# Attention operands without the norm row, head 1 in block form, two weight chunks split by an adding transfer

## The chip, the cores and the metric

One core of a Trainium2 chip. The metric is the device time of one execution in microseconds (us), median over runs. In the rows PE is TensorE (PEld its weight loads), DVE VectorE, ACT ScalarE, POOL GpSimd, SP SyncE; SPq, ACTq and POOLq are the DMA queues that SP, ACT and POOL issue to. L12 is line 12 of the kernel; one line's number differs a little between the kernel before and the changed one.

## The reference, cut to what matters

512 tokens of 1024 features, float32, two layers: dilated attention and a SwiGLU FFN, then a pooling mixer and a SwiGLU FFN, a root-mean-square norm ahead of each. The change touches the attention only:

```python
def rmsnorm(x, g):
    y = x * lax.rsqrt(jnp.mean(x * x, axis=-1, keepdims=True) + RMS_EPS)
    return y * g

# mixer A, h = rmsnorm(x, g): 8 heads of 128, three groups with (window, dilation)
#   (128, 1), (512, 4), (2048, 16); each group has its own q, k, v
qkv = (h @ w_qkv).reshape(B, S, 3, 3, 8, 128)
for g in range(3):
    o[g], lse[g] = dilated_window_attention(q[g], k[g], v[g], window, dil, slopes[g])
    # s = q k^T / sqrt(128) - slope * distance, masked; p = softmax(s); o = p v
wts = softmax(lse over the three groups)
out = sum(wts * o) @ w_out ; x = x + out
```

The norm's factor per token, 1 / sqrt(mean(x^2) + eps), is called the row here. q, k and v are linear in h, so it may be applied to x ahead of the product or to the result behind it.

## The kernel before

x stands transposed: eight tiles `X[c]` of 128 features by 512 tokens. A float32 product is made of two float32r parts of each factor, high and low (`split`: high part by ScalarE at L92, low part by VectorE as the difference at L93), and three matmuls: high by high, high by low, low by high.

**Plain products** (`Product`, matmuls at L329, L330, L332): one output chunk of 128 x 512 takes 8 feature chunks by three matmuls of 128x512. L332 is the one that reads the weights' low part. **Block form** (`seven`, matmuls in `mult` at L461 to L463): two output chunks at once from seven products of half-size blocks, 7 x 4 x 3 = 84 matmuls of 128x256, whose results VectorE adds together at L502 to L516. Its operands are sums of blocks of h, kept in `T` and made by `normed` and `prepare`. The weights of a block-form pair (`Pair`) come in two whole raw tiles and a half, one of which gets the fourth corner added by a transfer from GpSimd's queue (L173); sums of blocks are made by VectorE (L189, L190). A plain chunk with `lean` (used later in the kernel, L146 to L149) has its low part made otherwise: ScalarE writes the high part, then minus the high part, and a transfer on GpSimd's queue adds the weight from memory to that.

**The start.** x and the first weights (`w_first`) arrive chunk by chunk; the four lead products (L933, 96 matmuls) follow them on operands `U` without the row (x times the gain `nrm`). Squares of x are summed by TensorE (L411), VectorE forms `var` (L414), GpSimd takes the power (L417, `rcol`, per-token scalars on partitions), and `spread` (TensorE, L424) with an ACT copy (L942) makes `rows["row"]`, the row on all partitions. Meanwhile two further plain chunks of head 0 (`begin`) run. `prepare(k)` makes the block-form operands from x times gain times row, after the row is there. Of 24 qkv pairs most are in block form; head 0 is plain (6 q/k chunks, 2 v chunks), and so are head 1's first two groups (`NSOLO`).

**A head.** For each group g `seven` makes q and k; steps of earlier heads run between its products (`between`): `scores0` (group 0, L719), `scores12` (groups 1 and 2, L736, L740, L743), `scatter`, `merge` (weights `co` of the three groups; s0 scaled by DVE at L783, s12 by ACT at L786), `turn0` and `turn12` (transposes), `output` (L841, 30 small matmuls per head). v of two heads comes at once: group 0 in even heads (turned by `turn_values`), groups 1 and 2 in odd heads (`values12`). After head 7 the plain and block-form products with `w_out` follow, with `output` of heads 6 and 7 among them.

Loads are issued on SP's queue in the order of use, from rings of tiles (`raw` 4, `w` 5, `half` and `rawhalf` 2); `pump` splits the next weights. A scheduler orders each engine's instructions; on each engine they run in that order.

Of the kernel before, what the change touches and what calls it, by code (L numbers as in the profile page):

```python
# [8 lines left out]
F32 = mybir.dt.float32  # L9
# [6 lines left out]
P = 128  # L16
S = 512
# [25 lines left out]
NSOLO = 2  # L43
# [22 lines left out]
def trunk(ctx: ExitStack, tc: tile.TileContext, xT, xN, norms, w_first, w_qk, w_qkp, w_v0, w_v0p, w_v12, w_out, w_outp, w_pair, w_down, w_dblock, w_pin, w_pgrp,  # L66
# [173 lines left out]
    for h in range(HEADS):  # L240
        if h == 0:
            plain(*[w_qk[u] for u in range(len(QK) - NF)])
        for g in range(3):
            if h == 1 and g < NSOLO:
                plain(*[w_qk[len(QK) - NF + 2 * g + c] for c in range(2)])
            elif h:
                pairs(w_qkp[3 * h - 3 - NSOLO + g])
        if h == 0:
            plain(w_v0[0], w_v0[1])
        elif h % 2 == 0:  # L250
            pairs(w_v0p[h // 2 - 1])
        else:
            pairs(w_v12[h // 2, 0], w_v12[h // 2, 1], shift=APART)
# [216 lines left out]
    def seven(T, one, two, scratch, after={}, blocks=False):  # L470
# [44 lines left out]
        nc.vector.tensor_sub(into(two), p45, again(sums[:, :H2]))  # L515
        nc.vector.tensor_sub(into(one, right), sums[:, H2:], p45[:, H2:])  # L516
        behind(6)
# [56 lines left out]
    def normed(layer, k, row, h, t, chained=False):  # L574

        for i in range(2):
            c = k + i * K2
            nc.vector.scalar_tensor_tensor(h.t[:, i * S:(i + 1) * S], X[c], nrm[:, layer, c:c + 1], row,
                                           op0=OP.mult, op1=OP.mult)
# [20 lines left out]
    with tc.tile_pool(name="opool", bufs=1) as opool:  # L600
        early = [opool.tile([P, 2, S], F32R, tag=f"o{k}", name="early") for k in range(K2)]
        with tc.tile_pool(name="apool", bufs=1) as apool:
# [6 lines left out]
            def scaled_by(t, p, blocks):  # L609
                nc.vector.tensor_mul(by_block(t) if blocks else t, p, rows["row"])  # L610

            def evac(h, u, p):
                g, c = QK[u]
                t = apool.tile([P, S], F32, name=f"qk{g}{c}")
                scaled_by(t, p, g == 0)
                QKV[h, g, c] = t

            def values12(after={}):
# [59 lines left out]
                behind(6)  # L678
                return t
# [3 lines left out]
            def turn_values(h):  # L683

                t = apool.tile([P, NT, 2 * P], F32, name="v0")
                for c in range(2):
                    p = ps()
                    for b in range(NT):
                        nc.tensor.transpose(blk(p, b), blk(VT[c], b), ident)
                    nc.scalar.copy(t[:, :, c * P:(c + 1) * P], p.rearrange("p (b d) -> p b d", b=NT))  # L690
# [5 lines left out]
            def scores0(h):  # L696
# [12 lines left out]
                for blocks, bias in (((1, 2, 3), b0[:, :G]), ((0,), b0[:, G:])):  # L709
                    p = ps()  # L710
                    for i, b in enumerate(blocks):
# [6 lines left out]
                    n = len(blocks)  # L718
                    nc.vector.scalar_tensor_tensor(  # L719
                        s0[:, blocks[0]:blocks[0] + n], p[:, :n * G].rearrange("p (a k) -> p a k", a=n), SCALE,  # L720
                        bias[:, None].to_broadcast([P, n, G]), op0=OP.mult, op1=OP.add)
# [7 lines left out]
            def scores12(h):  # L729
# [4 lines left out]
                p, n = ps(), ps()  # L734
                for r in range(NT):
                    nc.tensor.matmul(blk(p, r), blk(QKV[h, 1, 0], r), blk(QKV[h, 1, 1], r), start=True, stop=True)  # L736
                for r in range(NT):
                    for j in range(NT):
                        c = slice(j * NI, (j + 1) * NI)
                        nc.tensor.matmul(n[c, r * NI:(r + 1) * NI], blk(QKV[h, 2, 0], r)[:, c], blk(QKV[h, 2, 1], r)[:, c],  # L740
                                         start=True, stop=True)
                for b, p, k in ((b12[:, :P], p, slice(0, P)), (b12[:, P:], n[:, :P], slice(P, G))):
                    nc.vector.scalar_tensor_tensor(  # L743
                        s12[:, :, k], p.rearrange("p (r k) -> p r k", r=NT), SCALE,
                        b[:, None, :].to_broadcast([P, NT, b.shape[1]]), op0=OP.mult, op1=OP.add)
# [15 lines left out]
            def merge(h):  # L761
# [20 lines left out]
                for b in (1, 2, 3, 0):  # L782
                    nc.vector.tensor_scalar(s0[:, b], s0[:, b], co[:, 0, b:b + 1], None, op0=OP.mult)  # L783
# [47 lines left out]
            def output(h):  # L831
# [21 lines left out]
                for r in range(NT):  # L853
# [4 lines left out]
            late = [apool.tile([P, S], F32R, tag=tag, name="early") for tag in ("t0", "o0")]  # L858
            late12 = apool.tile([P, 2, S], F32R, tag="t12", name="early")
            latev = apool.tile([P, 4, S], F32R, tag="v12", name="early")  # L860
            U = ([(early[k][:, 0], early[k][:, 1]) for k in range(K2)]
                 + [(latev[:, 2 * k], latev[:, 2 * k + 1]) for k in range(2)]
                 + [(late12[:, 0], late12[:, 1]), tuple(late)])
            H, T, o = {}, {}, []
# [667 lines left out]
```

## Time and profile before

| | |
|---|---|
| median of 3 runs | 1185.67 us (1185.33 to 1185.95) |
| the profiled execution | 1186.22 us, span 1184.4 us, clock 0.999 |
| busy: PE, DVE, ACT, POOL | 1175.3, 984.0, 721.8, 171.0 us |
| attention | to about 430 us; the rest is output projection, FFNs and the pooling mixer |
| DMA | 207.57 MB, mean 175 GB/s |

The page's group rows read: line, engine, operation, output from input, count, then busy time, the mean of one in ns, and the idle time before it with what ended it. A timeline row reads: start, duration, engine, line, operation, and in brackets how long the engine had been idle and what released it. A row with "from to" windows gives the length, and for each engine its busy time and instruction count, then the granted clock, the DMA share and GB/s.

### The profile page before, as it was taken

What the parts mean: (1) busy time and instruction counts of PE and PEld (TensorE: products, weight loads), DVE (VectorE), ACT (ScalarE), POOL (GpSimd) and SP (SyncE); (2) the same over time, 40 slices, a digit from 0 to 9 for tenths busy, and PEclk for the clock granted to TensorE, in tenths of its full rate; (3) what the DMA queues carried; (4) which work ended last, traced back from release to release, by engine and by line L of the source; (5) the groups of instructions that cost most, each with busy time, mean ns of one, the idle gap of its engine ahead of it and who ended that gap; (6) DMA issues with size and microseconds to landing.
All of it is one profiled execution on the core that took longest, in us unless ns stands there. A gap on an engine that the chain in (4) does not pass through costs nothing.

```text
span 1184.4 us, 25169 instructions
## 1 busy us (share of the span) xinstructions
PE 1175.3 (99%) x10042; PEld 1120.1 (95%) x10042; DVE 984.0 (83%) x1725; ACT 721.8 (61%) x1262; POOL 171.0 (14%) x165
## 2 busy tenths in 40 slices
PE   9999999999999999999999999999999999999997
PEld 7889999999999989889999999988889999999997
DVE  7997898879789878699988988656789998898875
ACT  6554554546455557747756775775575776676553
POOL 1101111111111002311111111122130111111100
PEclk9999999999999999999999999999999999999999
DMA  8537667665766557957777777798595777777732
GB/s 299 133 96 186 147 154 166 168 160 149 194 145 163 146 156 198 252 104 202 189 190 193 195 197 199 195 266 207 121 203 111 189 193 202 194 192 192 198 91 72
DMA packets 83766, 207.57 MB, mean 175 GB/s; under 512 B 7856, under 2 KB 13120, under 8 KB 83648
## 3 DMA queue, kind: packets, MB, share of 16 engines
q1 hardware_dynamic: 52672, 144.84, 36.4%
q0 software_dynamic: 30688, 60.83, 31.6%
q8 instruction: 78, 1.28, 0.4%
q14 instruction: 40, 0.33, 0.1%
q10 hardware_dynamic: 288, 0.29, 0.1%
HBM read 203.84 MB, written 2.10 MB: 174 GB/s over the span
## 4 chain that ended last, share of the span: by engine, by line
PE 96%; DMA 2%; issue 1%; DVE 1%; ACT 0%; POOL 0%; POOLq 0%; DVEq 0%; ACTq 0%
PE ps L461 21%; PE ps L463 20%; PE ps L462 20%; PE ps L329 7%; PE ps L330 7%; PE ps L332 7%; PE ps L841 2%; PE ps L933 2%; PE ps L632 2%; PE ps L634 2%; PE ps L633 2%; DMA raw<-w_outp 1%; PE ps L716 1%; PE ps L736 1%; PE ps L424 0%
## 5 line engine op out<-in xcount | busy, mean ns | idle before, releaser
L92 ACT ACTIVATE w<-raw 128x1024 fp32r<-128x1024 f32 x268 | 283.6, 1063 | 172.7 <-PE ps L463 67.5
L93 DVE TENSOR_TENSOR w<-raw,w 128x1024 fp32r<-128x1024 f32 x268 | 326.4, 1222 | 55.3 <-ACT w L92 51.2
L461 PE MATMUL ps<-far,w 128*128 128x256 f32 x896 | 246.5, 275 | 0.0
L462 PE MATMUL ps<-far,w 128*128 128x256 f32 x896 | 246.5, 275 | 0.0
L463 PE MATMUL ps<-far,w 128*128 128x256 f32 x896 | 246.4, 275 | 0.0
L461 PE MATMUL ps<-near,w 128*128 128x256 f32 x676 | 190.5, 282 | 0.0
L462 PE MATMUL ps<-near,w 128*128 128x256 f32 x676 | 186.9, 277 | 0.0
L463 PE MATMUL ps<-near,w 128*128 128x256 f32 x676 | 186.9, 276 | 0.0
L462 PEld LDWEIGHTS ps<-far,w 128*128 128x128 f32 x896 | 168.2, 188 | 0.1
L461 PEld LDWEIGHTS ps<-far,w 128*128 128x128 f32 x896 | 168.2, 188 | 0.1
L463 PEld LDWEIGHTS ps<-far,w 128*128 128x128 f32 x896 | 168.2, 188 | 0.0
L461 PEld LDWEIGHTS ps<-near,w 128*128 128x128 f32 x676 | 127.1, 188 | 0.5
L462 PEld LDWEIGHTS ps<-near,w 128*128 128x128 f32 x676 | 127.1, 188 | 0.0
L463 PEld LDWEIGHTS ps<-near,w 128*128 128x128 f32 x676 | 127.0, 188 | 0.0
L329 PE MATMUL ps<-near,w 128*128 128x512 f32 (+1 forms) x316 | 119.4, 379 | 0.0
L332 PE MATMUL ps<-near,w 128*128 128x512 f32 (+1 forms) x316 | 118.7, 376 | 0.0
L330 PE MATMUL ps<-near,w 128*128 128x512 f32 (+1 forms) x316 | 118.7, 376 | 0.0
L173 POOL DMA_DIRECT2D raw<-w_pair x36 | 43.6, 1210 | 296.5 <-DMA raw<-w_pair 131.8
L329 PEld LDWEIGHTS ps<-near,w 128*128 128x128 f32 x316 | 59.3, 188 | 10.9 <-ACT near L92 0.4
L332 PEld LDWEIGHTS ps<-near,w 128*128 128x128 f32 x316 | 59.3, 188 | 10.9
L330 PEld LDWEIGHTS ps<-near,w 128*128 128x128 f32 x316 | 59.5, 188 | 10.7 <-DVE near L93 0.2
L92 ACT ACTIVATE half<-rawhalf 128x512 fp32r<-128x512 f32 x84 | 52.8, 630 | 14.0 <-PE ps L463 11.8
(328 smaller groups left out, 2784.8 us busy)
## 6 DMA issues: line engine op xcount, KB each, us to landing
raw<-w_pair SPq DMA_DIRECT2D x80, 512.0 KB, 5.0
raw<-w_qkp SPq DMA_DIRECT2D x38, 512.0 KB, 4.6
raw<-w_pair POOLq DMA_DIRECT2D x36, 512.0 KB, 7.6
raw<-w_dblock SPq DMA_DIRECT2D x32, 512.0 KB, 4.5
raw<-w_qkp POOLq DMA_DIRECT2D x19, 512.0 KB, 7.6
raw<-w_v SPq DMA_DIRECT2D x18, 512.0 KB, 4.5
rawhalf<-w_pair SPq DMA_DIRECT2D x36, 256.0 KB, 5.2
raw<-w_dblock POOLq DMA_DIRECT2D x16, 512.0 KB, 7.4
```

Of the source, the lines that this page charges most:

```text
L92: nc.scalar.activation(hi, v, AF.Copy)
L93: nc.vector.tensor_tensor(lo, v, hi.bitcast(F32), op=OP.subtract)
L173: nc.gpsimd.dma_start(self.b.rearrange("p (a c) -> p a c", a=2), self.src[:, None, 3 * n:].to_broadcast([P, 2, n]), accum_op=OP.add)
L329: nc.tensor.matmul(self.p[:, cols], w[0][:, s], mh[:, cols], start=self.done == 0, stop=False)
L330: nc.tensor.matmul(self.p[:, cols], w[0][:, s], ml[:, cols], start=False, stop=False)
L332: nc.tensor.matmul(self.p[:, cols], w[1][:, s], mh[:, cols], start=False, stop=self.done == self.n)
L461: nc.tensor.matmul(dst, w.t[0][:, c], th, start=k == 0 and not on, stop=False, skip_group_check=on)
L462: nc.tensor.matmul(dst, w.t[0][:, c], tl, start=False, stop=False, skip_group_check=on)
L463: nc.tensor.matmul(dst, w.t[1][:, c], th, start=False, stop=k == n - 1, skip_group_check=on)
L632: nc.tensor.matmul(o, mh, wh, start=k == 0, stop=False)
L633: nc.tensor.matmul(o, mh, wl, start=False, stop=False)
L634: nc.tensor.matmul(o, ml, wh, start=False, stop=k == K2 - 1)
```

## The change

- Operands without the row. `U` (the leads' operands, high and low of x times gain) serve as the block-form operands for T11, T21 and T22; `prepare` no longer splits h (two chunks of it a call, four calls), and scales x on ScalarE (L576) with no wait for the row. `prepare(0)` moves ahead of `rstd`.
- The row is multiplied in behind the products. The second output of `seven` (k, or the second v chunk) by VectorE (L513, new, with the subtraction at L511 now in place); the first (q) not at all: its factor goes into the scale of the scores, per-token scalars `rk`, so that the scores' scale and bias takes four VectorE operations of 128x160 each instead of one or two larger ones (L721, L746). v of group 0 is scaled in `turn_values`' copies, v of groups 1 and 2 by four ScalarE operations of 128x512 in place (L680).
- `rk` is made from `rcol` by eight tiny ScalarE copies (L948) and, in the other order of tokens, by four one-column matmuls (L944) from `line`, a ScalarE copy of one partition of the row (L942).
- Head 1's groups 0 and 1 and the v pair of heads 0 and 1 go to block form; the plain weights `w_v0` and two plain pairs of `w_qk` are gone.
- The two plain q/k chunks of head 0 are `lean`: low part by ScalarE and an adding transfer.
- The scaling of s0 in `merge` goes from VectorE to ScalarE (L785).

```diff
-            plain(*[w_qk[u] for u in range(len(QK) - NF)])
+            plain(*[w_qk[u] for u in range(len(QK) - NF)], lean=True)
 ...
-        nc.vector.tensor_sub(into(two), p45, again(sums[:, :H2]))
         nc.vector.tensor_sub(into(one, right), sums[:, H2:], p45[:, H2:])
+        nc.vector.tensor_sub(p45 if row is not None else into(two), p45, again(sums[:, :H2]))
+        if row is not None:
+            nc.vector.tensor_mul(into(two), p45, row)
 ...
+            if row is None:
+                nc.scalar.activation(h.t[:, i * S:(i + 1) * S], X[c], AF.Copy, scale=nrm[:, layer, c:c + 1])
 ...
             def evac(h, u, p):
-                nc.vector.tensor_mul(by_block(t) if blocks else t, p, rows["row"])
+                if c:
+                    nc.vector.tensor_mul(v, p, rows["row"])
+                else:
+                    nc.scalar.copy(v, p if g else p.rearrange("p (y x z) -> p y x z", y=Y16, z=2))
 ...
             def values12(after={}):
+                for r in range(NT):
+                    nc.scalar.activation(t[:, r], t[:, r], AF.Copy, scale=rk[:, 1, r:r + 1])
 ...
             def scores0(h, ...):
-                    nc.vector.scalar_tensor_tensor(
-                        s0[:, blocks[0]:blocks[0] + n], ..., SCALE, ...)
+                    for i, b in enumerate(blocks):
+                        nc.vector.scalar_tensor_tensor(s0[:, b], p[:, i * G:(i + 1) * G], rk[:, 2, b:b + 1], bias,
+                                                       op0=OP.mult, op1=OP.add)
 ...
             def merge(h):
                 for b in (1, 2, 3, 0):
-                    nc.vector.tensor_scalar(s0[:, b], s0[:, b], co[:, 0, b:b + 1], None, op0=OP.mult)
+                    nc.scalar.activation(s0[:, b], s0[:, b], AF.Copy, scale=co[:, 0, b:b + 1])
 ...
             def prepare(k):
-                h, t = normed(0, k, rows["row"], Room(), Temp())
-                for i in range(2):
-                    held["h", k + i * K2], b = slot("h")
-                    H[k + i * K2] = b[:, 0], b[:, 1]
-                    split(*H[k + i * K2], h.t[:, i * S:(i + 1) * S])
-                T["11", k] = halves_of(*H[k])[0]
-                T["21", k], T["22", k] = halves_of(*H[k + K2])
+                h, t = normed(0, k, None, Room(), Temp())
+                T["11", k] = halves_of(*U[k])[0]
+                T["21", k], T["22", k] = halves_of(*U[k + K2])
 ...
+            lead += begin(1, 0, range(2))
+            prepare(0)
             rcol = rstd([acc[0]])
-            lead += begin(1, 0, range(3))
+            lead[-1].add(range(2, 5))
             nc.scalar.activation(rows["row"], spread(rcol), AF.Copy)
-            lead[-1].add(range(3, KC))
+            lead[-1].add(range(5, KC))
+            p, line = ps(), scratch("line")
+            nc.scalar.copy(line[:1].rearrange("p (x y z) -> p x y z", y=Y16, z=2), in_a_row(rows["row"][:1]))
+            for b in range(NT):
+                nc.tensor.matmul(p[:, b:b + 1], blk(line, b)[:1], ones[:1], start=True, stop=True)
+            for i, scale in ((0, 1.0), (2, SCALE)):
+                nc.scalar.activation(rk[:, i], p[:, :NT], AF.Copy, scale=scale)
+                for t, c in enumerate(rcol):
+                    nc.scalar.activation(rk[:, i + 1, t:t + 1], c, AF.Copy, scale=scale)
 ...
-            for h in range(1, HEADS):
-                for g in range(3):
+            for h in range(HEADS):
+                for g in range(3 if h else 0):
 ...
-                        seven(T, QKV[h, g, 0], QKV[h, g, 1], scratch, between(h, g), g == 0)
+                    seven(T, QKV[h, g, 0], QKV[h, g, 1], scratch, between(h, g), g == 0, rows["row"])
```

How the order of the instructions changes, at the places that the prediction speaks of. First GpSimd's queue at the start, before (`b` tiles are the scores' bias, `var` the mean square, `rcol` its power):

```order
L702 TENSOR_SCALAR b_492<-const 128x320
L705 TENSOR_SCALAR b_494<-const 128x128
L705 TENSOR_SCALAR b_494<-const 128x32
L417 TENSOR_TENSOR rcol<-var,nhalf 128x2 x2
L173 DMA raw<-w_qkp 128x2x512
L173 DMA raw<-w_v 128x2x512
```

The same queue in the changed kernel:

```order
L705 TENSOR_SCALAR b_518<-const 128x320
L708 TENSOR_SCALAR b_520<-const 128x128
L708 TENSOR_SCALAR b_520<-const 128x32
L148 DMA w<-w_qk 128x1024
L172 DMA raw<-w_v0p 128x2x512
L148 DMA w<-w_qk 128x1024
L172 DMA raw<-w_qkp 128x2x512
L412 TENSOR_TENSOR rcol<-var,nhalf 128x2 x2
```

Four transfers stand ahead of the power that gives the row, where none did.

VectorE around `var` at the start, before (`sq` sums of squares, `w` low parts of plain chunks):

```order
L384 TENSOR_TENSOR sq<-sq 128x512 x2
L93 TENSOR_TENSOR w<-raw,w 128x1024 x4
L414 TENSOR_SCALAR var<-ps 128x4
L93 TENSOR_TENSOR w<-raw,w 128x1024
L578 SCALAR_TENSOR_TENSOR room<-x,nrm,row 128x512 x2
```

And in the changed kernel (`temp`, `near` block sums of the operands; `raw<-raw` differences of the v0 pair's weights):

```order
L92 TENSOR_TENSOR near<-temp,near 128x512 x2
L92 TENSOR_TENSOR w<-raw,w 128x1024
L92 TENSOR_TENSOR half<-rawhalf,half 128x512
L188 TENSOR_TENSOR raw<-raw 128x512
L582 TENSOR_TENSOR temp<-room 128x2x256
L92 TENSOR_TENSOR w<-raw,w 128x1024
L409 TENSOR_SCALAR var<-ps 128x4
L189 TENSOR_TENSOR raw<-raw 128x512
```

`var` now stands behind a subtraction (L188) that reads the tile to which GpSimd's second transfer adds.

ScalarE in the attention's tail, before (`ex` the merge's exponentials, `s` scores, `oh`, `near`, `half` operands and weights of the output projection):

```order
L777 ACTIVATE ex<-ex 128x16
L92 ACTIVATE w<-raw 128x1024 x2
L92 ACTIVATE oh<-room 128x512
L786 ACTIVATE s_5242<-s_5242,co 128x160 x4
L92 ACTIVATE half<-rawhalf 128x512 x2
L92 ACTIVATE near<-room 128x512
L855 COPY o<-ps 128x512
```

And in the changed kernel:

```order
L779 ACTIVATE ex<-ex 128x16
L91 ACTIVATE w<-raw 128x1024 x2
L785 ACTIVATE s_5244<-s_5244,co 128x160 x4
L788 ACTIVATE s_5473<-s_5473,co 128x160 x4
L680 ACTIVATE v_5445<-v_5445,rk 128x512 x4
L91 ACTIVATE oh<-room 128x512
L91 ACTIVATE half<-rawhalf 128x512 x2
L91 ACTIVATE near<-room 128x512
L857 COPY o<-ps 128x512
```

Eight more operations stand between the second weight chunk and `oh`, among them the scaling of the values that `output` reads.

More of the change, by code (lines that the diff above doesn't have):

```diff
@@ L241, in trunk @@
         if h == 0:
-            plain(*[w_qk[u] for u in range(len(QK) - NF)])
+            plain(*[w_qk[u] for u in range(len(QK) - NF)], lean=True)
         for g in range(3):
[L244 to L251, printed above, removed]
+            if h:
+                pairs(w_qkp[3 * h - 3 + g])
+        if h % 2 == 0:
+            pairs(w_v0p[h // 2])
         else:
@@ L468, in part, with seven @@
         return unit.w[name]
-    def seven(T, one, two, scratch, after={}, blocks=False):
+    def seven(T, one, two, scratch, after={}, blocks=False, row=None):
         (unit,), = units.popleft()
@@ L600, in trunk @@
     with tc.tile_pool(name="opool", bufs=1) as opool:
-        early = [opool.tile([P, 2, S], F32R, tag=f"o{k}", name="early") for k in range(K2)]
         with tc.tile_pool(name="apool", bufs=1) as apool:
@@ L855, in output @@
                 nc.scalar.copy(o[h], po)
[L858 to L864, printed above, removed]
+            U, T, o = {}, {}, []
             class Room:
```

96 lines of the change are left out of this document (39 added, 57 removed).

## The prediction

> **What bounds the kernel now.** I read the page first, then the waits of TensorE's queue, then one stretch of two attention heads.
>
> ```profile
> span 1184.4 us, 25169 instructions
> PE 1175.3 (99%) x10042; PEld 1120.1 (95%) x10042; DVE 984.0 (83%) x1725; ACT 721.8 (61%) x1262; POOL 171.0 (14%) x165
> PE 96%; DMA 2%; issue 1%; DVE 1%; ACT 0%; POOL 0%; POOLq 0%; DVEq 0%; ACTq 0%
> PE ps L841 <- ACT t L808: 1.4, 1, 1.4
> PE ps L913 <- DVE idle L910: 1.2, 1, 1.2
> 131.60:233.80 102.20, 102.20 (x1115) 101.54 (x1105) 84.70 (x151) 53.81 (x106) 16.32 (x16) 1.00 0.67 163
> ```
>
> PE (TensorE) is 99% busy, the chain that ended last is 96% PE, and PE has two waits worth naming, both small. Two heads (131.6 to 233.8) take 102.2 us, all of it PE, with VectorE at 84.7, ScalarE at 53.8, and a granted clock of 1.00. So a matmul less is time less, and every new wait of PE is time more: nothing after it makes up for it.
>
> **The change: matmuls.** Three pairs of output chunks (head 1's first two groups, the v0 chunks of heads 0 and 1) go from plain (48 matmuls of 128x512) to block form (84 of 128x256).
>
> ```profile
> 416.15 0.39 PE L329 MATMUL ps<-oh,w 128*128 128x512 f32 x1
> 420.03 0.39 PE L332 MATMUL ps<-near,w 128*128 128x512 f32 x1
> 180.29 0.28 PE L461 MATMUL ps<-near,half 128*128 128x256 f32 x1
> 190.83 0.28 PE L632 MATMUL ps<-w,near 128*128 128x256 f32 x1
> ```
>
> The first two are the ends of a run of 18 plain matmuls: 3.88 us over 17 steps, 0.228 each. The other two stand 93 steps apart: 10.54 us, 0.1133 each. A pair falls from 48 x 0.228 = 10.95 to 84 x 0.1133 = 9.52 us; three pairs give 4.3 us. This is certain as long as PE is fed. Nine transposes or score matmuls more or less don't show; the four small matmuls that make `rk` (L944, one row by 128 columns) have no row in before: nearest is 32 of the sum's 128x1 in 0.43 us (next fence), so 0.05 to 0.5; I take 0.25, since they come in a switch of operands.
>
> **The front.** These are the rows around the first products.
>
> ```profile
> 5.43 22.08 PE L933 MATMUL ps<-early,w 128*128 128x512 f32 x96
> 18.16 0.64 ACT L382 ACTIVATE sq<-x 128x512 f32<-128x512 f32 x1
> 18.70 1.99 ACT L92 ACTIVATE w<-raw 128x1024 fp32r<-128x1024 f32 x2
> 27.44 0.43 PE L411 MATMUL ps<-ones,sq 128*32 128x1 f32 x32
> 27.95 0.16 DVE L414 TENSOR_SCALAR var<-ps 128x4 f32<-128x4 f32 x1 [2.00 <-PE ps L411]
> 28.20 2.23 POOL L417 TENSOR_TENSOR rcol<-var,nhalf 128x2 f32<-128x2 f32 x2 [7.76 <-DVE var L414]
> 28.37 0.39 PE L332 MATMUL ps<-early,w 128*128 128x512 f32 x1
> 29.98 1.21 PE L424 MATMUL ps<-ident,rcol 128*128 128x128 f32 x8
> 30.94 0.48 PE L329 MATMUL ps<-early,w 128*128 128x512 f32 x1
> 31.22 0.60 ACT L942 ACTIVATE row<-ps 128x512 f32<-128x512 f32 x1 [2.62 <-PE ps L424]
> L147 ACT ACTIVATE w<-w 128x1024 fp32r<-128x1024 f32 x32 | 33.6, 1055 | 0.6
> DMA to landing us min/median/max: 5.8/8.2/13.7
> raw<-w_v POOLq DMA_DIRECT2D x1, 512.0 KB, 7.1
> 24.72 1.22 DVE L93 TENSOR_TENSOR w<-raw,w 128x1024 fp32r<-128x1024 f32 x1 [0.23 <-ACT w L92]
> ```
>
> The first leads run until 27.5 and PE goes straight on. The fifth product's weights are split at 18.70 by ScalarE, and their low part by VectorE (1.22 a chunk), long before. Now that low part is made by ScalarE writing minus the high part (1.06, the L147 row, where the kernel does so already) and a transfer issued on GpSimd's queue that adds the weight (L148). ScalarE starts it later too, behind a new scaled room and a zeroed tile (128x512 each, 0.54 to 0.64 by the rows at 18.16 and 18.70): 18.70 + 1.15 = 19.85, high and low part done at 21.9, transfer issued then. Landing of such adding transfers (call it L): the line with the minimum, of the L149 transfers later in the kernel, says 5.8 to 13.7, median 8.2; the one of a v chunk in the first 60 us took 7.1. I take L = 7.6, between the two.
>
> 1. The third matmul of the fifth product (L327) needs it, two matmuls after the leads' end, at 27.9, and all later matmuls stand behind it: a wait of 21.9 + L - 27.9 = 1.6.
> 2. GpSimd issues behind it (23.0) the adding transfer of the v0 pair, which also lands after L. VectorE subtracts from what it brings (L188) ahead of `var` (L409): about half of 1.22 each for that and the temp, 1.22 for a chunk's low part, so `var` starts at 23.0 + L + 2.5 instead of 27.95. From `var` to the end of the spread matmuls was 2.97 (27.95 to 30.94, all in the rows). PE has 1.36 us more work before the spread than it had (six more plain matmuls): it would have been through at 32.3. Now 25.5 + L + 3.0 = 36.1, so 3.8 later in all, wait 1 included.
> 3. The `rk` matmuls wait for `line`, a copy of the row's first partition. On ScalarE, between `rcol` and `line`: eight tiny `rk`, a chunk's high part (1.06), two 128x512 splits, the row (0.60), a room (0.6), the copy (at most 0.6), some 4.7 us; PE has the spread and nine matmuls ahead of it, 2.5 us. A further wait of 2.0, between 1.2 (were the small ones free) and 2.8.
>
> Front: 3.8 + 2.0 + 0.25 = 6.05, or L - 1.55. While PE stands there, VectorE and ScalarE gain slack, but PE cannot make it up. What the operands save elsewhere (the row's split of eight h tiles, 0.6 to 0.7 each on both engines) lies beside PE work.
>
> GpSimd's queue order is the heart of this. The Trainium skill, "DMA: Bandwidth & Descriptors", section "Anatomy of one DMA — SWDGE (gpsimd) path", fits such a transfer as 2.0 us plus bytes over 436e3, 3.2 us for 512 KB (my estimate from it). By that, wait 1 would be nil and wait 2 too; the rows (5.8 at the least, 7.1 here) disagree with it by a factor of two.
>
> **Through the heads.** The place to watch is an odd head's scores of groups 1 and 2, where PE reads the second output of a pair soon after it is made; the rows are of such a place.
>
> ```profile
> 191.97 0.68 DVE L515 TENSOR_TENSOR qk<-ps,sums 128x512 f32<-128x512 f32 x1
> 192.57 0.41 DVE L516 TENSOR_TENSOR qk<-sums,ps 128x256 f32<-128x256 f32 x1
> 193.60 1.05 PE L736 MATMUL ps<-qk,qk 128*128 128x128 f32 x8
> 194.58 0.46 PE L740 MATMUL ps<-qk,qk 128*32 128x32 f32 x32
> ```
>
> Per pair of heads VectorE gets six row multiplications (0.68 as in the first row) and some 1.2 of smaller splits of its score operations, less eight scalings of 0.23 to 0.3 that ScalarE takes (L783 in the next fence): about +3 on 84.7. ScalarE gets those eight, four 128x512 scalings for an odd head's values and twice four smaller ones: about +6 on 53.8. Of 102.2, both stay beside PE. The second output was ready at 192.6. After the change the order is 0.34, 0.6, 0.69: ready at 193.6 to 194.2, with the group-2 matmuls at 194.6. I price it at nothing; were the cover gone, it is up to 0.6 for each of four odd heads.
>
> **The tail of the attention (head 7).** Here the last two output steps stand before plain products.
>
> ```profile
> 408.84 11.57 DMA raw<-w_outp
> 415.45 0.93 DVE L783 TENSOR_SCALAR s<-s,co 128x160 f32<-128x160 f32 x4
> 418.03 0.69 DVE L677 TENSOR_TENSOR v<-ps,sums 128x512 f32<-128x512 f32 x1
> 420.26 3.51 PE L841 MATMUL ps<-t,v 128*128 128x128 f32 x30
> 420.48 1.06 ACT L92 ACTIVATE w<-raw 128x1024 fp32r<-128x1024 f32 x1 [6.46 <-DMA raw<-w_outp]
> 421.44 0.61 ACT L92 ACTIVATE oh<-room 128x512 fp32r<-128x512 f32 x1
> 421.96 1.37 ACT L786 ACTIVATE s<-s,co 128x160 f32<-128x160 f32 x4
> 423.24 1.14 ACT L92 ACTIVATE half<-rawhalf 128x512 fp32r<-128x512 f32 x2
> 422.71 0.69 DVE L93 TENSOR_TENSOR oh<-room,oh 128x512 fp32r<-128x512 f32 x1
> 426.40 0.43 DVE L1034 TENSOR_TENSOR room<-room,o 128x256 f32<-128x256 f32 x1
> 430.19 3.67 PE ps L841 x30
> ```
>
> ScalarE sits 6.46 us on a chunk whose adding transfer takes 11.57 us to land. In the changed order that chunk stands ahead of four scalings of s0 (L785, VectorE's L783 before), four of s12 (L788) and four of the values (L680, new). From 420.48: chunk to 421.44, two stretches of 1.28 to 424.0, four 128x512 at 0.52 to 426.1 (425.1 if the scalings run closer). Output 6 needs the values after 14 of its 30 matmuls, at 421.8, so PE stands there. `oh`, behind them on ScalarE, goes from 421.44 to 426.1; VectorE's chain after it (oh, a half, a sum, four transposes, L1023, which was L1034) starts at 426.75 instead of 422.71 and reaches L1023 at 429.8 instead of 426.40, and output 7 (L841, at 430.19) hangs on that by the same steps as before. Later by 2.4 to 3.4; I take 2.9. If the transfer lands as in the L149 row (8.2), ScalarE is through before and it costs 0.3.
>
> **The sum.** -4.3 + 6.05 + 2.9 = +4.65, on the profiled execution's 1186.22 us, which is 0.55 above the median: 1190.9 there, 1190.3 as a median.
>
> **Rivals.** (a) The short landing, on the faster side: the adding transfers land in under 3.8 us, and waits 1 and 2 are nil. Front 2.25, tail 0.3: -1.75; with the wait for `line` also covered (its low end 1.2 and the tiny operations hidden), -3.7. So 1182 to 1184, taken as 1182.6. For it speaks only that page's fit; against it that no row goes below 5.8. It decides where L is under 3.8 and the `line` wait under 1.6. (b) Half covered: L at its least, 5.8, and the tail's transfer ahead of need: -4.3 + 4.25 + 0.3 = +0.25, 1185.9. For it: the front's queue holds only two adding transfers by then, and the 11.57 at the tail was with eight loads of x beside it. (c) VectorE decides in the heads: the second outputs come late for the scores, 4 x 0.6 = 2.4 more, 1192.7. For it, 87.6 of 102.2 and a margin of nearly nothing; against it, VectorE waits for ScalarE in between. (d) The block form gives nothing because its weights come late (PE would show waits on L456 to L458 in head 1): +4.3, 1194.6. Against it: 102.2 of 102.2 busy in the same form.
>
> **Chances.** Within 0.2% (2.4 us) is what a measurement here cannot tell from no change. Forecast 0.56, (a) 0.07, (b) 0.24, (c) 0.10, (d) 0.03. Faster 0.07 is (a); same 0.25 is (b) with a little of the forecast's lower end; slower 0.68. The forecast's own range is L from 7.1 to 8.2 and the tail from 0.3 to 3.4: 1187.2 to 1191.4. The 80% range goes from the middle of (a)'s upper edge, 1184, to between (c) and (d), 1194.
>
> **What the changed profile shows.** Waits of PE: a row of L327 on the transfer of w_qk near 1.6; one of the spread (L419) near 2.2; one of L944 on ScalarE's `line` near 2; L843 at the tail on ScalarE's L680 some 3. If L944's and L419's rows are missing, step 2 or 3 is wrong; if PE's windows of two heads grow past 102.2 by over 0.5, (c) is at work. The prediction goes wrong above all if the landing is not near 7.6, on which it hangs one for one.

## The result, and the profile after

The changed kernel takes 1200.26 us (median of 4, 1199.55 to 1201.55), the kernel before 1185.81 in the same runs: ratio 1.0124, 95% interval 1.0106 to 1.0141. It is 14.5 us slower; 4.6 were forecast. The page of the changed kernel, against the rows shown of before:

```profile
span 1199.8 us, 25528 instructions
PE 1180.0 (98%) x10158; PEld 1125.4 (94%) x10158; DVE 993.6 (83%) x1745; ACT 753.5 (63%) x1343; POOL 174.4 (15%) x170
PE 83%; DVE 7%; DMA 6%; issue 2%; ACT 1%; POOL 1%; DVEq 0%; SPq 0%; POOLq 0%; ACTq 0%
```

The chain that ended last, 96% PE before, now runs through VectorE and transfers for 13% of the span. What PE waits for (the waits of its queue: in total, times, longest):

```profile
PE ps L327 <- DMA w<-w_qk: 5.3, 1, 5.3
PE ps L743 <- DVE qk L513: 1.6, 2, 0.9
PE ps L944 <- ACT line L942: 1.5, 1, 1.5
PE ps L843 <- ACT v L680: 1.3, 1, 1.3
PE ps L905 <- DVE idle L902: 1.2, 1, 1.2
PE ps L843 <- ACT t L810: 1.0, 1, 1.0
PE ps L419 <- POOL rcol L412: 0.8, 2, 0.7
```

All the places of the prediction are there, the first three times its size. Two windows, the wait of L327 and what follows it (busy time of PE, PEld, DVE, ACT, POOL, then granted clock, DMA share, GB/s):

```profile
27.50:33.40 5.90, 0.60 (x4) 0.18 (x2) 0.69 (x1) 1.81 (x3) 1.21 (x1) 0.90 1.09 254
33.40:38.90 5.50, 5.50 (x43) 4.09 (x44) 2.31 (x3) 2.31 (x4) 0.00 (x0) 0.50 1.10 229
```

PE is busy all of the second window, but at a granted clock of 0.50. Start by start, 128x512 matmuls there stand 0.427 us apart instead of 0.228. The DMA engines are full (share over 1) while they move 229 to 254 GB/s; before, with loads alone, the same stretch moved 347 to 400 (26.9 to 29.4 us, share 1.02). The rows on GpSimd's queue, VectorE and PE there:

```profile
22.22 1.07 POOL L148 DMA_DIRECT2D w<-w_qk  x1 [1.60 <-ACT w L146]
22.98 1.59 POOL L172 DMA_DIRECT2D raw<-w_v0p  x1
33.40 0.80 PE L327 MATMUL ps<-near,w 128*128 128x512 f32 x1 [5.30 <-DMA w<-w_qk]
36.59 0.69 DVE L188 TENSOR_TENSOR raw<-raw 128x512 f32<-128x512 f32 x1 [7.78 <-DMA raw<-w_v0p]
38.94 0.15 DVE L409 TENSOR_SCALAR var<-ps 128x4 f32<-128x4 f32 x1
45.57 1.05 PE L944 MATMUL ps<-ones,line 1*128 1x1 f32 x8 [1.53 <-ACT line L942]
46.55 0.50 PE L324 MATMUL ps<-near,w 128*128 128x512 f32 x1
```

The first adding transfer, issued at 22.22, releases PE 11.1 us later; the second, issued at 22.98, releases VectorE at 36.5, after 13.5.

**Where the 15.4 us of span went.** Output 0 starts 9.6 us later than before, output 6 13.85, output 7 15.5, and from there to the end the distance stays at 15.4. So the loss lies wholly in the attention. The 48th plain matmul behind the leads starts at 51.90 instead of 39.66, so 12.2 us are lost in the front. From there to output 0, where the three pairs stand, only 2.6 of the 4.3 saved come back, so heads 0 and 1 lose 1.7 if the 4.3 is right. Heads 2 to 7 lose 4.2 and the tail 1.7.

### The profile page after: what moved, and what is told of

It reads as the page before. It is cut to its first block, busy times and chain, and to the rows that moved or that the text cites. A ratio compares the mean times of both kernels' runs of the same rounds, so it can differ in the third digit from the quotient of the medians.

```text
span 1199.8 us, 25528 instructions
## 1 busy us (share of the span) xinstructions
PE 1180.0 (98%) x10158; PEld 1125.4 (94%) x10158; DVE 993.6 (83%) x1745; ACT 753.5 (63%) x1343; POOL 174.4 (15%) x170
## 4 chain that ended last, share of the span: by engine, by line
PE 83%; DVE 7%; DMA 6%; issue 2%; ACT 1%; POOL 1%; DVEq 0%; SPq 0%; POOLq 0%; ACTq 0%
PE ps L456 19%; PE ps L458 18%; PE ps L457 18%; PE ps L324 6%; PE ps L327 6%; PE ps L325 6%; DMA raw<-w_v 2%; PE ps L843 2%; DVE w L92 2%; PE ps L632 2%; PE ps L634 2%; PE ps L633 2%; DMA raw<-w_v0p 1%; DMA raw<-w_outp 1%; DVE half L92 1%
## 5 line engine op out<-in xcount | busy, mean ns | idle before, releaser
L92 DVE TENSOR_TENSOR w<-raw,w 128x1024 fp32r<-128x1024 f32 x269 | 328.5, 1223 | 55.2 <-ACT w L91 50.9
L456 PE MATMUL ps<-far,w 128*128 128x256 f32 x896 | 246.5, 275 | 0.0
L458 PE MATMUL ps<-far,w 128*128 128x256 f32 x896 | 246.4, 275 | 0.0
L456 PE MATMUL ps<-near,w 128*128 128x256 f32 x749 | 210.9, 282 | 0.0
L458 PE MATMUL ps<-near,w 128*128 128x256 f32 x749 | 207.0, 276 | 0.0
L457 PE MATMUL ps<-near,w 128*128 128x256 f32 x749 | 206.9, 276 | 0.0
L456 PEld LDWEIGHTS ps<-far,w 128*128 128x128 f32 x896 | 168.2, 188 | 0.1
L458 PEld LDWEIGHTS ps<-far,w 128*128 128x128 f32 x896 | 168.2, 188 | 0.0
L456 PEld LDWEIGHTS ps<-near,w 128*128 128x128 f32 x749 | 140.7, 188 | 0.5
L457 PEld LDWEIGHTS ps<-near,w 128*128 128x128 f32 x749 | 140.8, 188 | 0.0
L458 PEld LDWEIGHTS ps<-near,w 128*128 128x128 f32 x749 | 140.8, 188 | 0.0
L327 PE MATMUL ps<-near,w 128*128 128x512 f32 (+1 forms) x332 | 126.1, 380 | 5.3 <-DMA w<-w_qk 5.3
L324 PE MATMUL ps<-near,w 128*128 128x512 f32 (+1 forms) x332 | 127.0, 383 | 0.0
L325 PE MATMUL ps<-near,w 128*128 128x512 f32 (+1 forms) x332 | 125.7, 378 | 0.0
L327 PEld LDWEIGHTS ps<-near,w 128*128 128x128 f32 x332 | 62.8, 189 | 17.4 <-DMA w<-w_qk 5.7
L325 PEld LDWEIGHTS ps<-near,w 128*128 128x128 f32 x332 | 63.0, 190 | 11.5 <-DVE near L92 0.2
L324 PEld LDWEIGHTS ps<-near,w 128*128 128x128 f32 x332 | 62.8, 189 | 11.6 <-ACT near L91 0.4
L188 DVE TENSOR_TENSOR raw<-raw 128x512 f32<-128x512 f32 x87 | 59.5, 684 | 10.7 <-DMA raw<-w_v0p 7.8
```

Of the source, the lines that this page charges most:

```text
L92: nc.vector.tensor_tensor(lo, v, hi.bitcast(F32), op=OP.subtract)
L188: nc.vector.tensor_add(a[:, :n], a[:, :n], b[:, :n])
L324: nc.tensor.matmul(self.p[:, cols], w[0][:, s], mh[:, cols], start=self.done == 0, stop=False)
L325: nc.tensor.matmul(self.p[:, cols], w[0][:, s], ml[:, cols], start=False, stop=False)
L327: nc.tensor.matmul(self.p[:, cols], w[1][:, s], mh[:, cols], start=False, stop=self.done == self.n)
L456: nc.tensor.matmul(dst, w.t[0][:, c], th, start=k == 0 and not on, stop=False, skip_group_check=on)
```

## The experiments

Times are medians; the control is the changed kernel, run once more with the second group.

**1. No adding transfers for the two plain chunks.**

```diff
-            plain(*[w_qk[u] for u in range(len(QK) - NF)], lean=True)
+            plain(*[w_qk[u] for u in range(len(QK) - NF)])
```

> Changed kernel, but the two plain chunks of head 0 have their low part made by VectorE as before (no adding transfers for them). Theory A (the late adding transfers at the front and the half clock behind the wait are most of the loss): the wait of L327 (5.3 us) and the slow matmuls behind it (about 3.2 us) go, 1190.5 to 1192.5. Rival B (var behind the subtraction L188 is what counts, the wait at L327 only stands ahead of it): var still waits for the v0 pair's adding transfer, the spread's wait grows to 4 us or more, 1194 to 1197. If transfers are slow because many are under way, the v0 pair's transfer lands in 8 to 9 us here instead of 13.5; if it is slow by itself, 13 us again.

1192.61 (ratio 1.0074, 1.0048 to 1.0100): 7.7 below the changed kernel. In the profiled execution L327 no longer waits and the clock stays at 1.00; the 48th plain matmul starts at 42.67 instead of 51.90, so 9.2 of the front's 12.2 us are gone. One of the five executions, not profiled, took 1200.51, with a mean clock of 0.995 where the others had 0.998 or 0.999. The spread waits 1.3:

```profile
PE ps L419 <- POOL rcol L412: 1.3, 1, 1.3
raw<-w_v0p POOLq DMA_DIRECT2D x1, 512.0 KB, 7.1
```

The v0 pair's transfer, alone on the queue, lands in 7.1 us (the last number of the DMA row), 13.5 in the changed kernel. Theory A holds; the transfer is not slow by itself. Nor do loads alone make it slow: four loads of pairs were issued on SP's queue while it was under way (22.6 to 27.9 us). What is gone from its side are the other adding transfers.

**2. The kernel before with nothing but those adding transfers** (the same line, the other way).

> Kernel before, with the two plain chunks of head 0 split by an adding transfer, nothing else. Theory A (transfers slow because others are under way, loads of whole chunks on SP's queue among them): landing 9 to 12 us, PE waits 3 to 5 us for the first, the clock falls to half for about 5 us, 1191 to 1194. Rival (the pair's adding transfers are what makes them slow): landing 7 to 8 us, wait 1 to 2 us, clock stays, 1187 to 1188.

1187.87 (ratio 1.0021, 1.0011 to 1.0030), 2.4 slower. Here two adding transfers are under way, and they land in 9.0 and 10.5 us; PE waits little, since the first is issued at 20.9, 1.3 us sooner than in the changed kernel, and lands at 29.9:

```profile
PE ps L332 <- DMA w<-w_qk: 1.3, 1, 1.3
w<-w_qk POOLq DMA_DIRECT2D x2, 512.0 KB, 9.7
```

The clock stays at 1.00 after 1.3 us. The landing is theory A's, the time the rival's. Landing against company: 7.1 us alone (run 1), 9.0 and 10.5 for two issued 2.0 us apart, 9.2 to 14.9 where four follow each other, in the changed kernel and each experiment that keeps them.

**3. Scores of odd heads one product later.**

```diff
-    values12({0: [later(scores12, h)], 4: [later(scatter, h)]})
+    values12({1: [later(scores12, h)], 4: [later(scatter, h)]})
```

(head 7 likewise)

> Changed kernel, but in odd heads the scores of groups 1 and 2 stand one product later (behind the second product of the values, not the first). Theory C (VectorE's row multiplication comes late for L743): the two waits of L743 on L513 (0.8 to 0.9 us each in heads 3 and 7) go, 1198.3 to 1199.0 and no PE wait on L513. Rival (the wait moves to a later step, the scatter or merge, since all steps come later): no change, 1200.

1193.84 (1.0075, 1.0060 to 1.0090), 6.6 below the control. More than expected: the waits on L513 are gone, and the ones of L843 at the tail too: the eight scalings now stand ahead of the late chunk on ScalarE, and from output 6 to output 7 the profile is 3.1 us shorter than the control's. The remaining 2 or so is the front, which came out better in this profile (L327 waits 1.6, and the half clock came behind the spread's wait instead, 38.2 to 41.6). So theory C holds for its 1.6; the tail came as a gift that the expectation did not have.

```profile
PE ps L419 <- POOL rcol L412: 3.4, 2, 3.2
PE ps L327 <- DMA w<-w_qk: 1.6, 1, 1.6
PE ps L905 <- DVE idle L902: 1.2, 1, 1.2
```

**4. Head 7's scalings on VectorE.** (Cut: the new lines are for head 7 only, the other heads keep the old ones.)

```diff
-                    nc.scalar.activation(t[:, r], t[:, r], AF.Copy, scale=rk[:, 1, r:r + 1])
+                    nc.vector.tensor_scalar(t[:, r], t[:, r], rk[:, 1, r:r + 1], None, op0=OP.mult)   # head 7
-                    nc.scalar.activation(s0[:, b], s0[:, b], AF.Copy, scale=co[:, 0, b:b + 1])
+                    nc.vector.tensor_scalar(s0[:, b], s0[:, b], co[:, 0, b:b + 1], None, op0=OP.mult)  # head 7
```

> Changed kernel, but for head 7 alone the scaling of s0 and of the values is on VectorE. Theory D (ScalarE's queue behind the late weight chunk holds up both outputs at the tail): the waits of L843 on L680 (1.3) and on the copies (1.0) shrink to what the kernel before had, 1.4 in all; 1198.5 to 1199.3. Rival (the late chunk of w_outp holds VectorE just as it held ScalarE): no change, 1200, or slower by up to 1.

1196.36 (1.0100, 1.0083 to 1.0117), 4.1 below the control and 2 lower than expected. Neither wait of L843 is left, not even the 1.4 of the kernel before: from output 6 to output 7 the profile is 3.1 us shorter than the control's. Theory D holds.

**5. The control.**

> The changed kernel itself, as the control for the runs beside it. If the landing of the adding transfers is what varies from one occasion to the next (11.1 us in the first profile, 9.0 to 9.3 in the three experiments that have them), this lands at 9 us too, waits 2 us at L327 and 3 us at the spread, and comes out at 1196 to 1198; if the earlier differences came from the edits alone, 1200 again.

1200.42 (1198.54 to 1204.13; 1.0132, 1.0110 to 1.0153), as at first, though its profile has L327 waiting 3.5 and the spread 1.8 (landing 9.3), and the half clock twice. The waits trade places from one execution to the next, and the front as a whole loses 10.6 us here, 12.2 in the first profile. So a difference of 2 us between two single profiles says nothing.

**6. Score matmuls grouped as before.**

```diff
-                for classes in ((0, 1, 2), (3,)):
-                    p = ps()
+                groups = [(ps(), (0, 1, 2)), (ps(), (3,))]
+                for p, classes in groups:      # all of group 1
 ...
+                for p, classes in groups:      # then all of group 2
```

> Changed kernel, with the score matmuls of groups 1 and 2 in the order of before: all of group 1, then all of group 2, instead of three classes and then the fourth. Theory E (each change of matmul shape costs PE 0.1 to 0.12 us twice, eight heads): two changes less a head, 0.34 x 8 = 2.7 us faster than the control. Rival (the gaps come from VectorE and from banks, not from the change of shape): within 0.5 of the control.

One of the four executions took 4208.5 us and is left out. The other three took 1196.52, 1196.87 and 1203.53 (ratio 1.0116, 1.0086 to 1.0146), which the control's 1.0132 doesn't differ from: no gain that can be told. In the profile, which is of the longest of the three, a row says what eats it: with the short matmuls together, PE comes to those that need the late second output.

```profile
PE ps L744 <- DVE qk L513: 4.1, 3, 2.9
```

Inconclusive for theory E alone (the changes of shape). Runs 9 and 11 settle it: in heads 2 to 7 nothing but this grouping differs between them, neither has a wait on L513's output there, and from output 0 to output 6 run 11 is 1.7 us shorter, 0.28 a head.

**7. var and power forced ahead of the transfers.** A small operation that reads the tile and `var` (on VectorE) or `rcol` (on GpSimd) stands ahead of L188's subtraction and of the fourth adding transfer, and the sum of squares ahead of the fifth product. (The diff is cut to the order and to VectorE's operation.)

```diff
+            rcol = rstd([acc[0]])
             lead += begin(1, 0, range(2))
             prepare(0)
-            rcol = rstd([acc[0]])
 ...
         def more(self):
+            if self in after_var:
+                nc.vector.tensor_add(tmp.tile([P, 1], F32, name="junk", bufs=1), a[:, :1], after_var[self][:, :1])
```

> Changed kernel with the sum of squares ahead of the fifth product, var forced ahead of the subtraction that reads the v0 pair's adding transfer, and the power forced ahead of the third adding transfer. Theory B' (var sits behind that landing): the spread's wait (3.1 us in the two last profiles) goes, the wait of L327 stays as in the control, 2 to 3.5 us faster than the control. Rival (the time only moves to L944, whose chain on ScalarE is as long as ever): 0 to 1.5 faster.

1220.68 (1.0298), 20 slower, the wrong way. Output 0 starts 0.6 us later than in the changed kernel's profile, 2.4 later than in the control's, no more; nearly all of the rest, 19.8 us, is lost behind output 7, where its matmuls of 128x256 are slower. The small operations wrote to two new tiles of 4 bytes. So it was run again (second run) with unused columns of `nhalf` in their place, and, third, the changed kernel with nothing but one such tile, never read:

> The edit of the run that forced var and the power ahead, this time without a tile of its own: the two small operations write into unused columns of a tile that is there. If that one run was slow because its two new 4-byte tiles moved all tiles behind them (its 128x256 matmuls took 118 ns instead of 114 everywhere), the matmuls are back at 114 ns and the time is 1196 to 1199: the spread's wait of 1.8 goes, but L944 waits about 3 for the line instead of nothing, and the first wait at L332 (3.5) with the half clock stays. If the order of the edit itself was at fault, 1220 again.

> Changed kernel with one more tile of 4 bytes a partition in the small pool, written once and never read. Theory G (where the tiles behind it stand decides how fast the block-form matmuls run): 128x256 matmuls at 117 to 118 ns, some 20 us slower than the control's 1200. Rival (tile addresses don't matter): within 2 us of the control, 1198 to 1202.

Without a new tile 1199.77; with the tile alone 1217.8 (1.0271, 1.0255 to 1.0286). Group rows of the tile run, and of the kernel with no new tile (the changed one):

```profile
L461 PE MATMUL ps<-far,w 128*128 128x256 f32 x896 | 250.8, 280 | 0.0
L459 PE MATMUL ps<-near,w 128*128 128x256 f32 x749 | 212.2, 283 | 0.0
```

```profile
L456 PE MATMUL ps<-far,w 128*128 128x256 f32 x896 | 246.5, 275 | 0.0
L456 PE MATMUL ps<-near,w 128*128 128x256 f32 x749 | 210.9, 282 | 0.0
```

Three far groups at 4.3 more and three near ones at 1.3 more make 16.8 of the 17.4 us. Theory G is shown. In time, 16.4 us of it lie behind output 7: start to start the 128x256 matmuls stand 116 to 118 ns apart there instead of 113, and within the attention 114. The run without it answers the question that was asked: `var` comes early, and the freed time turns into the wait for `line`.

```profile
PE ps L953 <- ACT line L951: 4.6, 1, 4.6
PE ps L332 <- DMA w<-w_qk: 2.8, 1, 2.8
```

So step 2 and step 3 are one chain: whichever of rows, spread and line PE meets last takes the wait.

**8. Idle matmuls in the waits.** To keep PE busy, on the kernel with var ahead: 24 of them before the fifth product, and then 9 before the rk matmuls.

```diff
+            for i in range(FILL):
+                nc.tensor.matmul(spare[:, :H2], idle[:, :P], idle, start=True, stop=True)
```

> The run above with 24 idle matmuls of 128x256 (2.7 us) placed into the time in which PE waits for the first adding transfer; they compute nothing that is used. Theory F (the clock is halved because PE stood still for over 3 us, and PE's slow matmuls cost 2 to 3 us behind the wait): the wait shrinks to about 1 us, the granted clock stays at 1.00 behind it, 1.5 to 3 us faster than the run above. Rival (the clock falls for another reason, as the load of the DMA engines): half clock as before, same time or slower by up to 1.

> The run with var and power forced ahead (1199.8), with nine idle matmuls of 0.427 us (3.8 us) ahead of the rk matmuls, in the time in which PE waited 4.6 us for the line. Nothing else is changed, and they compute nothing that is used. Theory F (the clock falls because PE stands still): the wait shrinks to about 1, the granted clock stays at 1.00 behind it, and the slow matmuls (seven at 0.427 instead of 0.227, the rk matmuls at half speed) go: 1197.3 to 1198.8. Rival (the clock falls for another reason): the same slow matmuls, 1199.5 to 1200.5.

The 24 were too many: they take 0.427 each, 10.2 us, and cost 5.2 (1204.93); but the clock stayed at 1.00 until PE's next stop. The 9 came out at 1199.92, no gain over 1199.77. Windows of that run, behind the first wait (2.3 us, not filled) and behind the filled place:

```profile
31.40:37.00 5.60, 5.60 (x13) 4.49 (x14) 1.25 (x3) 2.33 (x7) 0.51 (x1) 0.50 1.11 228
42.00:48.00 6.00, 6.00 (x31) 4.99 (x30) 6.00 (x11) 4.12 (x9) 1.23 (x1) 1.00 0.68 148
```

and of the unfilled run behind the same two places (waits of 2.8 and 4.6):

```profile
31.80:37.60 5.80, 5.79 (x29) 4.95 (x30) 1.51 (x3) 2.60 (x10) 0.17 (x1) 1.00 1.12 229
42.60:46.60 4.00, 4.00 (x13) 3.60 (x14) 3.91 (x7) 3.01 (x7) 1.23 (x1) 0.50 0.59 157
```

Where the wait was filled, the clock held; theory F is right at that place, and the DMA load (1.1 in both first windows) is not what halves it. But the half clock appeared behind the other wait instead, and once more at the tail (436.8 to 440.2), so the time is unchanged.

**9. All together, less the new tiles.** Low parts by VectorE (run 1), var ahead (run 7), scores later (run 3); a first version had the grouped order too, and the two 4-byte tiles.

> All edits that should pay together: low parts of the two plain chunks by VectorE, var and power forced ahead, the scores of odd heads one product later, the score matmuls grouped. The 4.3 us of matmuls stay, less 0.8 for the rk matmuls, about 1 for the front and 1 for the heads: 1182.5 to 1185 against 1185.4 before. Rival (the finer score operations and the later row keep costing what the matmuls save): 1185.5 to 1188.

> Low parts of the two plain chunks by VectorE, var and power forced ahead without a new tile, scores of odd heads one product later. If the new tiles were what made the first combined kernel slow: 114 ns matmuls, 1187 to 1190. Against before (1185.4): the matmuls' 4.3 less is eaten by the rk matmuls and the line (about 4) and by the shape changes in the heads (about 3).

1209.91 with the tiles, where 1182.5 to 1185 was expected, and 1190.9 without (1.0048, 1.0029 to 1.0066), still 5.3 slower than before; the wait for `line`, 2.7, and 3.4 us at half clock behind it are what stands out.

**10. The rk matmuls behind the sixth product**, in the changed kernel (the block of the diff from `line` to `rk` moved to after `prepare(3)`).

> Changed kernel with the rk matmuls and ScalarE's copies for them moved behind the sixth product (they are needed first by the scores of head 0). If the wait for line is a cost of its own where the transfers are late too: it costs up to 1.5 us in the control's state and this gains 1 to 2.5 (with the clock behind it), 1197.5 to 1199.5. Rival (with the transfers late, the line is there in time anyway): within 0.7 of the control's 1200.4.

1198.42 (1196.51 to 1199.31), 2.0 below the control, but its profiled execution is as long as the control's (spans 1196.3 and 1196.8), and in neither does L944 wait. Too close to settle.

**11. Run 9 with the grouped order and with run 10's move.**

> Low parts of the two plain chunks by VectorE, var and power forced ahead without a new tile, the rk matmuls behind the sixth product, scores of odd heads one product later, score matmuls grouped. Against the combined run without the last two or three of these (1190.9): the wait of 2.7 for the line with its clock goes (3 to 4 us) and the grouped matmuls save 2 to 2.7: 1184 to 1186.5, beside 1185.5 before: the same, or barely faster. If the grouped matmuls bring the waits for VectorE back, 1187 to 1188.

1185.23 (median of 11) against 1185.83: ratio 0.9999, interval 0.9990 to 1.0008. No difference from the kernel before, with every long wait taken out:

```profile
span 1183.0 us, 25528 instructions
PE ps L912 <- DVE idle L909: 1.2, 1, 1.2
PE ps L425 <- POOL rcol L418: 0.5, 2, 0.3
PE ps L463 <- DVE tx L92: 0.5, 1, 0.5
PE ps L778 <- DVE far L766: 0.3, 1, 0.3
```

It is 15 us faster than the change as made, and it wins nothing on the kernel before. The 48th plain matmul starts at 40.90 here, 1.2 us behind the kernel before instead of 12.2.

**12. The 4 bytes elsewhere.** The same tile in the kernel before, and a tile of 256 bytes in the changed one.

> Kernel before with the 4-byte tile added, written once and never read. If the shift by 4 bytes is what slows block-form matmuls: 128x256 matmuls at 117 ns instead of 113, 1200 to 1206. If only the changed kernel's layout is sensitive: 1185 to 1187.

> Changed kernel with a tile of 256 bytes a partition instead of 4. If the odd 4 bytes do the harm (operands and weights off a boundary): matmuls at 113 ns, 1198 to 1201. If any shift of the tiles against each other does it: 117 ns, 1215 to 1219.

1205.33 (before: 1185.43) and 1200.9 (control 1200.42). It is the odd 4 bytes, not any shift, and both kernels have it; sizes between 4 and 256 bytes were not tried.

## Why the prediction was wrong

The direction and the places were right, the sum was off by 10. By its own terms:

- **Matmuls, -4.3.** Not contradicted: 2.6 come back where the pairs stand, beside finer operations that cost, and run 11 removes the waits and ends level with before, though it carries the rk matmuls and the finer score operations. It was not measured by itself.
- **Step 1, L = 7.6.** This term failed. It was read from rows in which an adding transfer had the queue nearly to itself. Here four of them were issued within 8 us, beside six loads of pairs; L was 11.1, the wait 5.3 instead of 1.6. The front's windows with a DMA share over 1 show the crowd; runs 1 and 2 show it by subtraction and by dose. The landing of 13.7 at the upper end of the L149 line, and the 11.57 at the tail, were in the prediction's own rows; its range for L ended at 8.2. Rival (b) leaned on two adding transfers in the front's queue, but the third went out at 24.61, with the first two still under way.
- **Not in the sum: the half clock.** This is a term that the prediction left out. The first 11 matmuls behind the wait and a sum of squares take 5.66 us (33.40 to 39.06), in run 1 at full clock 3.08: 2.6 us more. The Trainium skill, "TensorE: Matmul & The Clock Gate", section "Part 1: The HAM clock gate", says the clock halves after about 3.4 us of an idle array and comes back after as much work, by a window that runs free, so that one program differs from run to run. By that rule a wait of 5.3 costs twice, and I could have priced it. Windows of the changed kernel, cut where its granted clock changes:

```profile
28.78:32.19 3.41, 0.00 (x0) 0.00 (x0) 0.03 (x1) 0.53 (x1) 1.21 (x1) 1.00 1.07 254
32.19:39.02 6.83, 5.62 (x43) 4.19 (x44) 2.42 (x5) 2.43 (x4) 0.00 (x0) 0.50 1.12 228
39.02:42.43 3.41, 2.56 (x14) 1.81 (x13) 1.95 (x6) 1.64 (x8) 2.01 (x2) 1.00 0.81 215
```

The rows agree on the window: behind a wait in the attention, every stretch at 0.50 in these profiles is 3.41 or 6.83 us long. They do not show 3.4 us of idling as a threshold. In each profile they also begin and end on one grid of 3.41 us. Of the stretches of that grid within the attention, those in which PE was busy for up to 0.39 were all followed by 0.50; those at 0.43 to 0.69 only sometimes. So a wait of 1.3 us halved the clock at the tail in run 8 (0.59 busy), and one of 2.8 left it alone in run 7 (0.63 and 0.54 in the two stretches that it touched).
- **Step 2.** `var` at 38.94 against 33.1 forecast, by the landing of the second transfer, 13.5 instead of 7.6. PE was so late already that it waited only 0.8 more here, 1.8 to 3.4 where step 1's wait was shorter.
- **Step 3.** 1.5 measured, 2.0 forecast. The rk matmuls took 1.0 (45.57 to 46.55), not 0.25 for all four: about 0.25 for each.
- **Through the heads, priced at nothing.** This failed too: 4.2 us in heads 2 to 7 and 1.7 in heads 0 and 1, rival (c) in part. The margin was read right and judged wrong. In head 3:

```profile
202.94 0.41 DVE L510 TENSOR_TENSOR qk<-sums,ps 128x256 f32<-128x256 f32 x1
203.27 0.68 DVE L92 TENSOR_TENSOR half<-rawhalf,half 128x512 fp32r<-128x512 f32 x1
203.87 0.69 DVE L511 TENSOR_TENSOR ps<-ps,sums 128x512 f32<-128x512 f32 x1
204.60 0.69 DVE L513 TENSOR_TENSOR qk<-ps,row 128x512 f32<-128x512 f32 x1
203.66 0.83 PE L739 MATMUL ps<-qk,qk 128*128 128x128 f32 x6
205.34 0.40 PE L743 MATMUL ps<-qk,qk 128*32 128x32 f32 x24 [0.85 <-DVE qk L513]
205.67 0.49 PE L739 MATMUL ps<-qk,qk 128*128 128x128 f32 x2
206.09 0.27 PE L743 MATMUL ps<-qk,qk 128*32 128x32 f32 x8
```

A weight's low part (L92, the half) slips in ahead of the two steps of the second output (L511, L513), and PE waits 0.85. The same rows show the order's other price: two forms of matmul in four pieces instead of two, where before one change of form was enough. Waits of this kind make 1.6 in all, and the pieces, by runs 9 and 11, another 1.7 in heads 2 to 7. The remaining 0.9 of the 4.2 stays unassigned; run 11 has it too.
- **Tail, +2.9.** 1.7 measured, and the mechanism as forecast: ScalarE held by the late chunk, then eight scalings, then `oh`.

```profile
422.55 9.59 DMA raw<-w_outp
432.21 1.06 ACT L91 ACTIVATE w<-raw 128x1024 fp32r<-128x1024 f32 x1 [4.39 <-DMA raw<-w_outp]
433.18 1.37 ACT L785 ACTIVATE s<-s,co 128x160 f32<-128x160 f32 x4
435.73 2.54 ACT L680 ACTIVATE v<-v,rk 128x512 f32<-128x512 f32 x4
437.10 2.61 PE L843 MATMUL ps<-t,v 128*128 128x128 f32 x16 [1.27 <-ACT v L680]
```

The chunk landed 9.6 us after its issue, not 11.6, so 2.0 sooner; the term came out 1.2 smaller, as ScalarE took 0.3 longer from the chunk's end to `oh` than forecast, and about 0.5 is not assigned. Runs 3 and 4 take this term away.

Rival (a) has no support: the quickest adding transfer of the first 60 us of any run took 6.4 us to land. By the fit of the Trainium skill, "DMA: Bandwidth & Descriptors", section "Anatomy of one DMA — SWDGE (gpsimd) path", 3.2 us for 512 KB as an estimate, there would have been no wait at L327; the measured 11.1 decides against it. Rival (d) has none either: no wait of PE on L456 to L458 stands among the changed kernel's.

What stays open: about 1 of the front's 12.2 us (5.3, 2.6, 0.8, 1.5 and 1.0 are assigned), the 1.7 of heads 0 and 1 in its parts, 0.9 in heads 2 to 7, and what decides on the clock when PE was busy for about half of a stretch.

## What to carry to other kernels

Price a transfer from rows with as much company as it will have, and a wait of TensorE twice, for itself and for the slow matmuls behind it (5.3 and 2.6 us here). Where one late input is put ahead of a chain (here the power behind two queues), removing it moves the wait to the next link, so take the links out together: runs 1, 3 and 4 gave 4 to 8 us each, run 10 some 2 that can't be told from the noise, run 7 less than 1, and only run 11 brought the kernel back. And ask, before moving work, what the best case would win: here 4.3 us of matmuls, against finer operations that cost as much.

## What the runs showed of the hardware that was not expected

- One unread tile of 4 bytes a partition, placed ahead of others, made the 128x256 matmuls 1 to 5 ns longer (275 to 280 and 282 to 283 ns in the rows) and the kernel 17.4 to 19.9 us slower, in both kernels, nearly all of it behind the attention; a tile of 256 bytes in the same place cost nothing (1200.9 against 1200.42).
- Four adding transfers and six loads together fill the DMA engines (share 1.10) at 229 GB/s, where loads alone moved 347 to 400 before at a share of 1.02.
- Behind a wait the clock was 0.50 for 3.41 or 6.83 us, and whether a wait of 1.3 to 2.8 us is enough differs between executions.
- An adding transfer of 512 KB took 7.1 us to land with loads alone beside it (run 1), 9.0 and 10.5 where two were issued 2.0 us apart (run 2), and 9.2 to 14.9 where four followed each other.
